# Attention inside a decoder block: the next pair of logit tiles issued ahead of the present pair's transposes, with the interleaving of the gate projection left to the scheduler

## The chip, the cores and the metric

The program runs on one core of one Trainium2 chip. A core has five engines that run their own instruction streams: TensorE (PE, with its weight loads listed as PEld), VectorE (DVE), ScalarE (ACT), GpSimd (POOL) and SyncE (SP), from which this kernel issues its DMAs. The metric is the device time of one execution in microseconds, lower is better.

## The reference

One decoder layer over a sequence of 1024 tokens of width 1024. The normed input is projected once; its columns feed three mixers (RWKV-7, a gated linear recurrence, dilated attention) and three merge gates.

```python
h = rms_norm(x, norm_mix_g)
z_a, z_bx, z_by, z_q, z_k, z_v, z_g = split_cols(h @ w_in, IN_SIZES)   # z_g: 3 * 1024 columns
y_a = rwkv7_mixer(z_a, ...) @ proj_a
y_b = rglru_mixer(z_bx, z_by, ...) @ proj_b
y_c = dilated_attention_mixer(z_q, z_k, z_v, q_g, k_g, rel_bias) @ proj_c
gates = sigmoid(z_g.reshape(bsz, seq, 3, D_MODEL))
x = x + (gates[:, :, 0] * y_a + gates[:, :, 1] * y_b + gates[:, :, 2] * y_c) @ w_out
x = x + square(relu(rms_norm(x, norm_mlp_g) @ mlp_up)) @ mlp_down
```

The attention has three groups g with dilations 1, 4 and 16, each with four heads of 64. A block of 128 queries sees its own 128 keys and the previous 128 of the same residue class.

```python
logits = einsum('brnqhe,brnkhe->brnhqk', qs, kb) + bias      # masked
m = max(logits);  p = exp(logits - m);  l = sum(p)
o = einsum('brnhqk,brnkhe->brnqhe', p, vb) / l;  lse = m + log(l)
# the three groups are then summed with softmax(lse) over the groups as weights
```

## The kernel before, in words

The stages follow one another: norm and projections, the linear recurrence, RWKV (to about 800 us of the profile), the attention together with the gate projection z_g (about 806 to 1140 us), the merge (products named `pj`), output projection, and the MLP. The change touches only the attention with the gate projection.

**Attention.** There are six units `(cc, g)`: two pairs of heads (`cc`) times three groups, in the order cc=0 with g=0,1,2, then cc=1. A unit has four tiles `sp` of 256 queries for two heads `h`. One tile is: the logits `l` on PE (L1029) into one PSUM bank per head; on DVE scale and bias into the SBUF tile `lg` (L1039), the row maxima `stat` (L1042, L1045) and their negation `nm` (L1046); on ACT the exponential in place in `lg` (L1048); on PE 128x128 transposes `pt` of `lg` (L1059); on ACT the copies `ptS` (L1063, L1067); on PE the product `o` with the values `vt` (L1074); on DVE the copy `og` (L1182). In the traces a name carries its indices: `l1110` is g=1, cc=1, sp=1, head 0. A unit's inputs are loaded by `load` (`z0`, `z1`, L998) and `prep` (`bias`, then the broadcast rows `rb`, which scale `z1` at L1012). At a unit's end `combine_rows` transposes the statistics (`stt`, L1083), stores them and reads them back as rows (L1091).

**Combination.** `combine(cc)` weighs and adds the three groups' outputs in halves: small 16-row work for the weights (L1102 to L1120), a store `cw_d` and broadcast loads `cb` (L121), `yc` = weight times og (L1138), `yt` (L1142), and POOL's `yc += yt` (L1143), then the store `yc_d` (L1145). For cc=0 all products run on POOL, during unit (1,0) and after it; for cc=1 they run on DVE at the end. The `yt` tiles use the same two buffers (tag "lg") as the logit tiles.

**Gate projection.** `gate_z` is a generator: each step gives out one product `zg` of twelve 128x512 matmuls (`mm3`, L236 to L238: three fp32r matmuls per k-tile). From the third pair n of column tiles on it uses a Strassen-Winograd scheme: seven products j in two PSUM banks, with operands `wz` made by ACT (L1313) and POOL or DVE (L1314) from the loads `wr_z` (L1293), sums of weights on DVE (L1308 to L1312), the combinations T1 to T4 of the activations (L1244 to L1253), and evacuation by an ACT copy (L1353), a DVE addition `th` (L1357) and a tanh on ACT with a store (L1281, L1282). `th_103` is n=10, j=3.

**Order.** The code is traced in Python, and a scheduler then orders each engine's instructions by a timeline that it simulates. `filler(n)` takes n more steps from `gate_z`; before the change each such step may not be scheduled ahead of the last logits matmul of the third tile back (`tc.issue_after(pins[-lag].ins)`). Buffers that matter: two PSUM banks for `l`, two for `pt`, one each for two `o`; two SBUF buffers for `lg` with `yt`, two for `rb` with `cb`; one each for `z0`, `z1`, `vt`, `bias`.

Of the kernel before, what the change touches and what calls it, by code (L numbers as in the profile page):

```python
# [18 lines left out]
P = 128  # L19
# [13 lines left out]
DILS = (1, 4, 8)  # L33
# [91 lines left out]
def hybrid_block(ctx, tc, io, out, dbg=None):  # L125
    nc = tc.nc
    V, A, G, S, PE = nc.vector, nc.scalar, nc.gpsimd, nc.sync, nc.tensor
    dbg = dbg or {}

    cp = ctx.enter_context(tc.tile_pool(name="cp", bufs=1))  # L130
    wp = ctx.enter_context(tc.tile_pool(name="wp", bufs=1))
    dr = ctx.enter_context(tc.tile_pool(name="dr", bufs=1, space=DRAM))
    pg = ctx.enter_context(tc.tile_pool(name="pg", bufs=2, space=PSUM))
# [192 lines left out]
    gt = gt_p.__enter__()  # L326
    h2_p = tc.tile_pool(name="hS", bufs=1, side="right")
    h2 = h2_p.__enter__()
    late = []
    fill = gate_z(tc, w_in, ht, h2, hp, gt, wp, pg, th_d, load_cols, mm3, late)  # L330
    ys = {}

    def load_y(src, b, ks, place, raw=None):
# [650 lines left out]
    return first  # L984


def attention(tc, io, dbg, psum, der, cg, yc_d, bias_d, sst, rk_d, cw_d, v_d, qk_d, fill):
# [4 lines left out]
    with tc.tile_pool(name="ac", bufs=1) as ac, tc.tile_pool(name="au", bufs=2) as au:  # L992
# [19 lines left out]
                V.scalar_tensor_tensor(kn[:, sl], kn[:, sl], gcol, rb, ALU.mult, ALU.mult)  # L1012
            stats[(cc, g)] = au.tile([P, 2, 2, 8], F32, tag="stat", name=f"stat{u}", bufs=4)

        def tiles(cc, g, sp, po):

            u = f"{g}{cc}"
            dil = DILS[g]
            q_, kn, rqk, vt = zt[(cc, g, 0)], zt[(cc, g, 1)], rqks[(cc, g)], vts[(cc, g)]
            bias, stat = biases[(cc, g)], stats[(cc, g)]  # L1020
            los = [0 if (dil == 1 and s > 0) or (dil == 4 and s % 2 == 1) else 128 for s in (2 * sp, 2 * sp + 1)]
            hs = [slice(64 * h, 64 * h + 64) for h in range(2)]
            same = los[0] == los[1]
            pls = [psum("s", 2, f"l{u}{sp}{h}") for h in range(2)]

            for q in range(2):
                s, lo = 2 * sp + q, los[q]
                for h in range(2):
                    mm = PE.matmul(pls[h][:, 256 * q + lo : 256 * q + 256], q_[hs[h], s * P : (s + 1) * P],  # L1029
                                   kn[hs[h], s * P + lo - 128 : (s + 1) * P], start=True, stop=True)  # L1030
            pins.append(mm)
            lgs = []
            for h in range(2):
                lg = au.tile([P, 2, 256], F32, tag="lg", name=f"lg{u}{sp}{h}")
                lgs.append(lg)
                nm = au.tile([P, 2], F32, tag="nm", name=f"nm{u}{sp}{h}")
                for q in range(2):
                    s, lo = 2 * sp + q, los[q]
                    V.scalar_tensor_tensor(lg[:, q, lo:256], pls[h][:, 256 * q + lo : 256 * q + 256], rqk[:, 8 * h + s : 8 * h + s + 1],  # L1039
                                           bias[:, h, lo:256], ALU.mult, ALU.add)  # L1040
                if same:
                    V.tensor_reduce(stat[:, 0, h, 2 * sp : 2 * sp + 2], lg[:, :, los[0] : 256], AX.X, ALU.max)  # L1042
                else:
                    for q in range(2):
                        V.tensor_reduce(stat[:, 0, h, 2 * sp + q : 2 * sp + q + 1], lg[:, q, los[q] : 256], AX.X, ALU.max)  # L1045
                V.tensor_scalar(nm, stat[:, 0, h, 2 * sp : 2 * sp + 2], -1.0, None, ALU.mult)  # L1046
                for q in range(2):
                    A.activation(lg[:, q, los[q] : 256], lg[:, q, los[q] : 256], AF.Exp, bias=nm[:, q : q + 1],  # L1048
                                 accum_out=stat[:, 1, h, 2 * sp + q : 2 * sp + q + 1])
            yield  # L1050
            ptSs = []
            for h in range(2):
                lg = lgs[h]
                pt = psum("w", 2, f"pt{u}{sp}{h}")
                ptS = au.tile([P, 2, 2, P], F32, tag="ptS", name=f"ptS{u}{sp}{h}")
                ptSs.append(ptS)
                for q in range(2):
                    for b in range(los[q] // 128, 2):
                        PE.transpose(pt[:, 256 * q + 128 * b : 256 * q + 128 * b + 128], lg[:, q, 128 * b : 128 * b + 128], ident)  # L1059
                p4 = pt.rearrange("p (q b t) -> p q b t", q=2, b=2)  # L1060
                if same:
                    b0 = los[0] // 128
                    A.copy(ptS[:, :, b0:2, :], p4[:, :, b0:2, :])  # L1063
                else:
                    for q in range(2):
                        b0 = los[q] // 128
                        A.copy(ptS[:, q, b0:2, :], p4[:, q, b0:2, :])  # L1067

            for q in range(2):
                s = 2 * sp + q  # L1070
                b0 = los[q] // 128
                for b in range(b0, 2):
                    for h in range(2):
                        PE.matmul(po[hs[h], q * P : (q + 1) * P], vt[:, s - 1 + b, hs[h]], ptSs[h][:, q, b, :], start=b == b0, stop=b == 1)  # L1074
# [86 lines left out]
        load(*units[0])
# [56 lines left out]
def gate_z(tc, w_in, ht, h2, hp, gt, wp, pg, th_d, load_cols, mm3, late):  # L1218


    nc = tc.nc
# [13 lines left out]
    def combinations():  # L1235
# [37 lines left out]
        for k in range(4):  # L1273
# [3 lines left out]
            if k % 2:  # L1277
                yield

    def done(b, m, hf, th, src):  # L1280
        A.activation(th, src, AF.Tanh, scale=0.5)  # L1281
        S.dma_start(th_d[b, m, :, hf * H : hf * H + H], th)  # L1282
# [56 lines left out]
    for n in range(n_plain, len(pairs)):  # L1339
# [5 lines left out]
        for j, (nm, bk, first) in enumerate((("B11", X, True), ("B21", Y, True), ("T2", X, False), ("T1", Y, True),  # L1345
# [1 line left out]
            if n == n_plain:  # L1347
                next(comb, None)
            wh, wl = ops.pop((n, j))
            mm3(bk, [(wh[:, k, :], wl[:, k, :], B[nm][0][:, k, :], B[nm][1][:, k, :]) for k in range(4)], first=first, skip=True)  # L1350
            if j in (0, 2, 3):
                t = tile(f"{n}{j}")
                A.copy(t, bk)  # L1353
# [431 lines left out]
```

## Time and profile before

| | |
|---|---|
| runs, us | 1974.58, 1969.91, 1969.65 (median 1969.91) |
| profiled execution, us | 1969.19 |
| its span, us | 1967.2 |
| granted TensorE clock, mean | 0.989 |
| PE busy | 1901.7 us, 97% of the span |
| PEld busy | 1511.0 us, 77% |
| DVE / ACT / POOL busy | 63% / 39% / 39% |

The profile covers one execution; its span lies 2.0 us under that execution's time. A busy share is the engine's time under instructions, and PE's matmuls overlap, so what a stage costs is read from the distance between the starts of matmuls and from PE's waits, not from the durations alone. L numbers are lines of the kernel before; the changed kernel's lines are up to 23 higher in this part.

### The profile page before, as it was taken

Reading aid. Unit: us, or ns where it says so; the run is one execution under the profiler, and the core shown is the slowest. Engines: PE = TensorE matmul, PEld = TensorE weight load, DVE = VectorE, ACT = ScalarE, POOL = GpSimd, SP = SyncE. Lnnn points to the kernel's source line nnn. Section 1 sums busy time; section 2 is a strip of 40 time slices with the busy share of each in tenths; the row PEclk is TensorE's granted clock in tenths of the full one; section 3 lists DMA queues with packets and bytes.
Section 4 is the critical chain, followed back from the end, with each engine's and each line's share of the span. In section 5 each row is a group of like instructions: output and inputs, shape, how many; then the busy total and the mean of one; then the engine's idle time right before and its main releaser. Section 6 shows DMA issues by size and latency. Waiting matters only on the chain. (4 is left out here: it accounts for less than half of the span.)

```text
span 1967.2 us, 29765 instructions
## 1 busy us (share of the span) xinstructions
PE 1901.7 (97%) x11634; PEld 1511.0 (77%) x11634; DVE 1245.2 (63%) x1992; ACT 761.9 (39%) x1275; POOL 773.5 (39%) x631
## 2 busy tenths in 40 slices
PE   8999999999999999999999999998999999999999
PEld 6776777787677878777767778887888888888887
DVE  5546356657656564775454566447776677987975
ACT  5675223233333331355545331145333233333332
POOL 1243424442352350442442352344344343444542
PEclk9999999999999999999999999999999999999999
DMA  4122322221221221424443574442444439535231
GB/s 148 54 61 78 93 52 59 59 60 51 55 70 41 64 66 37 134 92 135 129 147 119 173 267 159 177 172 107 161 150 153 158 141 386 195 133 190 89 129 64
DMA packets 191554, 236.53 MB, mean 120 GB/s; under 512 B 38472, under 2 KB 133349, under 8 KB 191414
## 3 DMA queue, kind: packets, MB, share of 16 engines
q1 hardware_dynamic: 191238, 234.62, 35.9%
q8 instruction: 91, 1.49, 0.3%
q14 instruction: 49, 0.40, 0.1%
q0 software_dynamic: 160, 0.02, 0.0%
q10 hardware_dynamic: 16, 0.00, 0.0%
HBM read 168.14 MB, written 68.82 MB: 120 GB/s over the span
## 5 line engine op out<-in xcount | busy, mean ns | idle before, releaser
L1505 POOL TENSOR_TENSOR wl_d<-dr,wh_d 128x1024 fp32r<-128x1024 f32 x40 | 101.3, 2532 | 126.9 <-ACT wh_d L1504 118.4
L1314 POOL TENSOR_TENSOR wz<-wr_z,wz 128x512 fp32r<-128x512 f32 x60 | 80.6, 1344 | 161.8 <-ACT wz L1313 147.6
L1505 DVE TENSOR_TENSOR du<-dq,du 128x1024 fp32r<-128x1024 f32 x56 | 126.1, 2251 | 23.3 <-ACT du L1504 22.7
L236 PE MATMUL dx<-wh_d,du 128*128 128x512 f32 x256 | 99.7, 389 | 0.4 <-DVE acc L1685 0.4
L237 PE MATMUL dx<-wl_d,du 128*128 128x512 f32 x256 | 99.6, 389 | 0.0
L238 PE MATMUL dx<-wh_d,du 128*128 128x512 f32 x256 | 99.4, 389 | 0.0
L1504 ACT CAST wh_d<-dr 128x1024 fp32r<-128x1024 f32 x40 | 42.1, 1052 | 141.7 <-PE dx L238 72.8
L788 DVE TENSOR_SCALAR s<-ac,wc 64x64 f32<-64x64 f32 x128 | 36.1, 282 | 66.7 <-PE ac L784 64.4
L1505 POOL TENSOR_TENSOR wl_a<-ur,wh_a 128x1024 fp32r<-128x1024 f32 x15 | 47.6, 3174 | 75.3 <-ACT wh_a L1504 75.3
L237 PE MATMUL g_z<-hl,wh_z 128*128 128x512 f32 x192 | 77.1, 402 | 0.0
L238 PE MATMUL g_z<-hh,wl_z 128*128 128x512 f32 x192 | 76.9, 401 | 0.0
L236 PE MATMUL g_z<-hh,wh_z 128*128 128x512 f32 x192 | 76.5, 398 | 0.4 <-DVE zsq L443 0.4
L1505 POOL TENSOR_TENSOR wl_s<-ur,wh_s 128x1024 fp32r<-128x1024 f32 x16 | 43.3, 2704 | 77.7 <-ACT wh_s L1504 77.7
L229 POOL TENSOR_TENSOR wl_wo<-wr_wo,wh_wo 128x1024 fp32r<-128x1024 f32 x16 | 38.7, 2416 | 62.6 <-ACT wh_wo L228 62.6
L1504 ACT CAST du<-dq 128x1024 fp32r<-128x1024 f32 x56 | 58.6, 1047 | 1.8 <-DMA dq<-u_d 1.8
L1048 ACT ACTIVATE lg<-lg,nm 128x128 f32<-128x128 f32 (+1 forms) x96 | 42.3, 443 | 42.0 <-DVE nm L1046 42.0
L1685 DVE TENSOR_TENSOR acc<-dx,acc 128x512 f32<-128x512 f32 x64 | 41.9, 679 | 25.1 <-PE dx L238 25.1
L236 PE MATMUL v<-wh_wv,hh 128*128 128x256 f32 x192 | 56.3, 293 | 1.2 <-DVE st L794 1.2
L236 PEld LDWEIGHTS dx<-wh_d,du 128*128 128x128 f32 x256 | 48.0, 188 | 10.8 <-DVE acc L1685 0.9
L238 PEld LDWEIGHTS dx<-wh_d,du 128*128 128x128 f32 x256 | 48.1, 188 | 10.1
L237 PEld LDWEIGHTS dx<-wl_d,du 128*128 128x128 f32 x256 | 48.0, 188 | 9.9
L237 PE MATMUL v<-wl_wv,hh 128*128 128x256 f32 x192 | 55.6, 290 | 0.0
(757 smaller groups left out, 6178.7 us busy)
## 6 DMA issues: line engine op xcount, KB each, us to landing
dq<-u_d SPq DMA_DIRECT2D x56, 512.0 KB
wr_z<-in_w_in_dram SPq DMA_DIRECT2D x32, 512.0 KB
ur<-in_mlp_up_dram SPq DMA_DIRECT2D x16, 1024.0 KB
dr<-in_mlp_down_dram SPq DMA_DIRECT2D x16, 1024.0 KB
th_d<-th SPq DMA_DIRECT2D x48, 256.0 KB
tg<-th_d SPq DMA_DIRECT2D x32, 256.0 KB
wr_wo<-in_w_out_dram SPq DMA_DIRECT2D x16, 512.0 KB
qk_d<-zo SPq DMA_DIRECT2D x24, 256.0 KB
```

What stands on the lines that cost most here:

```text
L229: E.tensor_tensor(lo, raw, hi, ALU.subtract)
L236: PE.matmul(ps, lh, rh, start=first and i == 0, stop=False, skip_group_check=skip)
L237: PE.matmul(ps, lh, rl, start=False, stop=False, skip_group_check=skip)
L238: end = PE.matmul(ps, ll, rh, start=False, stop=last and i == n - 1, skip_group_check=skip)
L788: V.tensor_scalar(ns[half[h], :], pb[h][half[h], 128 * j + 64 * c : 128 * j + 64 * c + 64], wc[half[h], 2 * i + c : 2 * i + c + 1], None, ...
L1048: A.activation(lg[:, q, los[q] : 256], lg[:, q, los[q] : 256], AF.Exp, bias=nm[:, q : q + 1], accum_out=stat[:, 1, h, 2 * sp + q : 2 * sp ...
L1314: (V if i == 2 else G).tensor_tensor(l, src, h, ALU.subtract)
L1504: A.copy(hi, src)
L1505: split.last = E.tensor_tensor(lo, src, hi, ALU.subtract)
L1685: V.tensor_tensor(acc[row][:, half[col]], ps, acc[row][:, half[col]], ALU.add)
```

## The change

The generator `tiles` is split into three functions. `logits(cc, g, sp)` holds the `l` matmuls, the DVE work and the exponentials, and leaves its `lg` tiles in a dictionary; `transposes` takes both `pt` banks and gives out all transposes before the copies `ptS`; `values` holds the `o` products. The loop traces `logits` of tile sp+1 ahead of `transposes` of tile sp. `load` and `prep` of the next unit move from behind tile 3 to behind the transposes of tile 2. `combine(0)` is made before the tile loop of unit (1,0) rather than behind its first tile. `filler` no longer pins its steps; it takes 2 steps at a unit's start, 1.2 behind each tile's transposes and 1.4 behind each of the first three `o` products, where it was 2 + 0.2 a tile and 3 at a unit's end. The dictionary `order` and the context `in_order()` are empty and record only the last matmul.

```diff
-        def filler(n, lag=3):
+        def filler(n):
             nonlocal owed
             owed += n
             while owed >= 1:
                 owed -= 1
-                with tc.issue_after(pins[-lag].ins) if len(pins) >= lag else nullcontext():
-                    next(fill, None)
+                next(fill, None)
...
+            logits(cc, g, 0)
+            filler(2)
+            if n == 3:
+                sums = combine(0)
             for sp in range(4):
-                po = psum(f"ac{sp % 2}", 1, f"o{g}{cc}{sp}")
-                for i, _ in enumerate(tiles(cc, g, sp, po)):
-                    filler(0.2 if i else 2)
-                    next(sums, None)
-                    next(sums, None)
-                V.tensor_copy(ogs[(cc, g)][:, sp * 256 : (sp + 1) * 256], po[:, 0:256])
-                if sp == 3 and n + 1 < 6:
+                if sp + 1 < 4:
+                    logits(cc, g, sp + 1)
+                ptSs = transposes(cc, g, sp)
+                if sp == 2 and n + 1 < 6:
                     load(*units[n + 1])
                     prep(*units[n + 1])
-                    filler(3)
-                if sp == 0 and n == 3:
-                    sums = combine(0)
+                filler(1.2)
+                next(sums, None)
+                po = psum(f"ac{sp % 2}", 1, f"o{g}{cc}{sp}")
+                values(cc, g, sp, ptSs, po)
+                V.tensor_copy(ogs[(cc, g)][:, sp * 256 : (sp + 1) * 256], po[:, 0:256])
+                if sp < 3:
+                    filler(1.4)
+                next(sums, None)
+                next(sums, None)
...
+        def transposes(cc, g, sp):
...
+            pts = [psum("w", 2, f"pt{u}{sp}{h}") for h in range(2)]
+            with in_order():
+                for h in range(2):
+                    for q in range(2):
+                        for b in range(los[q] // 128, 2):
+                            order["block"] = PE.transpose(pts[h][:, 256 * q + 128 * b : 256 * q + 128 * b + 128], lgs[sp][h][:, q, 128 * b : 128 * b + 128], ident)
```

Both programs hold the same number of matmuls. In the attention, PE's order before has 286 runs of one kind of matmul: 45 of `l`, 41 of `o`, 59 of `pt`, 134 of `zg` and 7 others. In the new order there are 252: 39, 36, 47, 123 and 7. Three places show what moves.

PE in unit (1,1), where the logits of its last tile `l113*` meet the values `o111` of its second tile. Before:

```order
L1074 MATMUL o111_9909<-ptS1110_9974,vt11_9819 64x128
L238 MATMUL zg70_9847<-hh11_95,wz75_9804 128x512
L1029 MATMUL l1130_10077<-z1_11_9740,z0_11_9738 128x128
L1029 MATMUL l1130_10077<-z1_11_9740,z0_11_9738 128x256
L1059 MATMUL pt1120_10055<-cg_102,lg1120_10001 128x128
L236 MATMUL zg71_9848<-zT4h_8485,wz76_9863 128x512
L237 MATMUL zg71_9848<-zT4l_8486,wz76_9863 128x512
L238 MATMUL zg71_9848<-zT4h_8485,wz76_9863 128x512
L1059 MATMUL pt1120_10055<-cg_102,lg1120_10001 128x128 x2
L236 MATMUL zg71_9848<-zT4h_8485,wz76_9863 128x512
L1029 MATMUL l1131_10078<-z1_11_9740,z0_11_9738 128x128
L1074 MATMUL o111_9909<-ptS1111_9981,vt11_9819 64x128
```

After, from the first `o111` that stands together with others:

```order
L1088 MATMUL o111_9971<-ptS1111_9950,vt11_9743 64x128
L1088 MATMUL o111_9971<-ptS1110_9947,vt11_9743 64x128
L1088 MATMUL o111_9971<-ptS1111_9950,vt11_9743 64x128
L1088 MATMUL o111_9971<-ptS1110_9947,vt11_9743 64x128
L1088 MATMUL o111_9971<-ptS1111_9950,vt11_9743 64x128
L1038 MATMUL l1131_10019<-z1_11_9595,z0_11_9593 128x128
L1038 MATMUL l1131_10019<-z1_11_9595,z0_11_9593 128x256
L1067 MATMUL pt1121_10043<-cg_102,lg1121_9930 128x128 x3
L236 MATMUL zg70_9892<-hh11_95,wz75_9881 128x512
L237 MATMUL zg70_9892<-hl11_96,wz75_9881 128x512
L238 MATMUL zg70_9892<-hh11_95,wz75_9881 128x512
L236 MATMUL zg70_9892<-hh11_95,wz75_9881 128x512
```

The logits and values that stood one or two at a time between `zg` matmuls now stand in longer runs, and the transposes `pt112*` of the third tile follow in fewer pieces.

DVE in the same unit, around the weight sum that needs the load `wr_z80` (L1308 and L1309 before, L1331 and L1332 after). Before:

```order
L1357 TENSOR_TENSOR th_70_9861<-zg70_9847,th_70_9861 128x512
L1039 SCALAR_TENSOR_TENSOR lg1110_9916<-l1110_9910,sst_84,bias11_9742 128x128
L1039 SCALAR_TENSOR_TENSOR lg1110_9916<-l1110_9910,sst_84,bias11_9742 128x256
L1308 TENSOR_TENSOR wr_z80_9866<-wr_z81_9868,wr_z80_9866 128x512
L1045 TENSOR_REDUCE stat11_9752<-lg1110_9916 128x1
L1039 SCALAR_TENSOR_TENSOR lg1111_9925<-l1111_9911,sst_84,bias11_9742 128x128
L1045 TENSOR_REDUCE stat11_9752<-lg1110_9916 128x1
L1039 SCALAR_TENSOR_TENSOR lg1111_9925<-l1111_9911,sst_84,bias11_9742 128x256
L1309 TENSOR_TENSOR wr_z81_9868<-wr_z81_9868 128x512
```

After:

```order
L1047 SCALAR_TENSOR_TENSOR lg1110_9816<-l1110_9810,sst_84,bias11_9597 128x128
L1047 SCALAR_TENSOR_TENSOR lg1110_9816<-l1110_9810,sst_84,bias11_9597 128x256
L1053 TENSOR_REDUCE stat11_9607<-lg1110_9816 128x1 x2
L1054 TENSOR_SCALAR nm1110_9817<-stat11_9607 128x2
L1380 TENSOR_TENSOR th_70_9906<-zg70_9892,th_70_9906 128x512
L1331 TENSOR_TENSOR wr_z80_9911<-wr_z81_9913,wr_z80_9911 128x512
L1332 TENSOR_TENSOR wr_z81_9913<-wr_z81_9913 128x512
L1047 SCALAR_TENSOR_TENSOR lg1111_9825<-l1111_9811,sst_84,bias11_9597 128x128
L1047 SCALAR_TENSOR_TENSOR lg1111_9825<-l1111_9811,sst_84,bias11_9597 128x256
```

The maxima and `nm` of `lg1110` now stand ahead of the sum that needs `wr_z80`; `lg1111` stands behind both sums.

DVE at the end of the attention, where `combine(1)` (`yc`, `yt`) meets the evacuations `th_100`, `th_103`, `th_102` of n=10. Before:

```order
L1357 TENSOR_TENSOR th_100_10626<-zg101_10613,th_100_10626 128x512
L1308 TENSOR_TENSOR wr_z110_10631<-wr_z111_10633,wr_z110_10631 128x512
L1309 TENSOR_TENSOR wr_z111_10633<-wr_z111_10633 128x512
L1138 TENSOR_TENSOR yc10_10713<-cb10_10661,og01_9318 128x512
L1311 TENSOR_TENSOR th_s11_10708<-wr_z110_10631,wr_z111_10633 128x512
L1312 TENSOR_TENSOR wr_z110_10631<-wr_z110_10631,th_s11_10708 128x512
L1142 TENSOR_TENSOR yt101_10733<-cb11_10666,og11_9818 128x512
L1314 TENSOR_TENSOR wz112_10705<-th_s11_10708,wz112_10705 128x512
L1357 TENSOR_TENSOR th_103_10703<-zg100_10612,th_103_10703 128x512
L1142 TENSOR_TENSOR yt102_10754<-cb12_10671,og21_10264 128x512
L1142 TENSOR_TENSOR yt111_10797<-cb11_10666,og11_9818 128x512
L1357 TENSOR_TENSOR th_102_10686<-zg101_10613,th_102_10686 128x512
```

After:

```order
L1380 TENSOR_TENSOR th_100_10647<-zg101_10634,th_100_10647 128x512
L1151 TENSOR_TENSOR yc10_10674<-cb10_10620,og01_9259 128x512
L1155 TENSOR_TENSOR yt101_10693<-cb11_10625,og11_9742 128x512
L1155 TENSOR_TENSOR yt102_10718<-cb12_10630,og21_10166 128x512
L1155 TENSOR_TENSOR yt111_10760<-cb11_10625,og11_9742 128x512
L1155 TENSOR_TENSOR yt112_10781<-cb12_10630,og21_10166 128x512
L1380 TENSOR_TENSOR th_103_10708<-zg100_10633,th_103_10708 128x512
L1331 TENSOR_TENSOR wr_z110_10652<-wr_z111_10654,wr_z110_10652 128x512
L1151 TENSOR_TENSOR yc11_10740<-cb10_10620,og01_9259 128x512
L1332 TENSOR_TENSOR wr_z111_10654<-wr_z111_10654 128x512
L1334 TENSOR_TENSOR th_s11_10713<-wr_z110_10652,wr_z111_10654 128x512
L1380 TENSOR_TENSOR th_102_10688<-zg101_10634,th_102_10688 128x512
```

`th_103` stood behind the weight sums of `wr_z110`, one `yc` and one `yt`; now it stands behind one `yc` and four `yt`, of which the last two wait for POOL to free a buffer, and the weight sums follow it.

On POOL the thirteen instructions from `yt001` to the last `yc01` addition keep their kinds. On SP the loads `cb010` and `cb011`, which stood ahead of the store of `th_60`, now stand behind it; the load `wr_z80`, with five DMAs between it and the store of `yc01` before, now follows that store directly; and both loads `wr_z110` and `wr_z111`, which stood around the first store `cw_d` of `combine(1)`, now follow all its stores `cw_d` and loads `cb`; the last store `cw_d`, which stood behind four `cb` loads, now stands ahead of them.

More of the change, by code (lines that the diff above doesn't have):

```diff
@@ L328, in hybrid_block @@
     h2 = h2_p.__enter__()
-    late = []
-    fill = gate_z(tc, w_in, ht, h2, hp, gt, wp, pg, th_d, load_cols, mm3, late)
+    late, order = [], {}
+    fill = gate_z(tc, w_in, ht, h2, hp, gt, wp, pg, th_d, load_cols, mm3, late, order)
     ys = {}
@@ L369, in hybrid_block @@
     late.append(load_first)
-    attention(tc, io, dbg, psum, der, cg, yc_d, bias_d, sst, rk_d, cw_d, v_d, qk_d, fill)
+    attention(tc, io, dbg, psum, der, cg, yc_d, bias_d, sst, rk_d, cw_d, v_d, qk_d, fill, order)
     yp_p = tc.tile_pool(name="yp", bufs=1)
@@ L984, in lru, with attention @@
     return first
-def attention(tc, io, dbg, psum, der, cg, yc_d, bias_d, sst, rk_d, cw_d, v_d, qk_d, fill):
+def attention(tc, io, dbg, psum, der, cg, yc_d, bias_d, sst, rk_d, cw_d, v_d, qk_d, fill, order):
     nc = tc.nc
@@ L1049, in tiles @@
                                  accum_out=stat[:, 1, h, 2 * sp + q : 2 * sp + q + 1])
-            yield
+        def transposes(cc, g, sp):
+            u = f"{g}{cc}"
+            los, hs, same = places(g, sp)
+            pts = [psum("w", 2, f"pt{u}{sp}{h}") for h in range(2)]
+            with in_order():
+                for h in range(2):
+                    for q in range(2):
+                        for b in range(los[q] // 128, 2):
+                            order["block"] = PE.transpose(pts[h][:, 256 * q + 128 * b : 256 * q + 128 * b + 128], lgs[sp][h][:, q, 128 * b : 128 * b + 128], ident)
@@ L1051, in tiles @@
             ptSs = []
             for h in range(2):
-                lg = lgs[h]
-                pt = psum("w", 2, f"pt{u}{sp}{h}")
                 ptS = au.tile([P, 2, 2, P], F32, tag="ptS", name=f"ptS{u}{sp}{h}")
                 ptSs.append(ptS)
-                for q in range(2):
-                    for b in range(los[q] // 128, 2):
-                        PE.transpose(pt[:, 256 * q + 128 * b : 256 * q + 128 * b + 128], lg[:, q, 128 * b : 128 * b + 128], ident)
-                p4 = pt.rearrange("p (q b t) -> p q b t", q=2, b=2)
@@ L1061, in tiles @@
[L1061 to L1074, printed above, removed]
@@ L1075, in tiles, with values @@
-            yield
+                p4 = pts[h].rearrange("p (q b t) -> p q b t", q=2, b=2)
+                for q in ([slice(0, 2)] if same else range(2)):
+                    b0 = los[0 if same else q] // 128
+                    A.copy(ptS[:, q, b0:2, :], p4[:, q, b0:2, :])
+            return ptSs
+        def values(cc, g, sp, ptSs, po):
+            los, hs, same = places(g, sp)
+            vt = vts[(cc, g)]
+            with in_order():
+                for q in range(2):
+                    s = 2 * sp + q
+                    b0 = los[q] // 128
+                    for b in range(b0, 2):
+                        for h in range(2):
+                            order["block"] = PE.matmul(po[hs[h], q * P : (q + 1) * P], vt[:, s - 1 + b, hs[h]], ptSs[h][:, q, b, :], start=b == b0, stop=b == 1)
@@ L1215, in bias_tiles, with gate_z @@
             S.dma_start(bias_d[g], bass.AP(tensor=src.tensor, offset=src.offset, ap=[[EW, 4], [0, P], [1, EW]]))
-def gate_z(tc, w_in, ht, h2, hp, gt, wp, pg, th_d, load_cols, mm3, late):
+def gate_z(tc, w_in, ht, h2, hp, gt, wp, pg, th_d, load_cols, mm3, late, order):
     nc = tc.nc
@@ L1278, in combinations, with products @@
                 yield
+    def products(*args, **kw):
+        with nullcontext():
+            order["fill"] = mm3(*args, **kw)
     def done(b, m, hf, th, src):
@@ L1327, in gate_z @@
                 for kh in range(2):
-                    mm3(ps, [(hi[:, 4 * kh + k, :], lo[:, 4 * kh + k, :], ht[(0, kh, hf)][:, k, :], ht[(1, kh, hf)][:, k, :]) for k in range(4)],
-                        first=kh == 0, last=kh == 1)
+                    products(ps, [(hi[:, 4 * kh + k, :], lo[:, 4 * kh + k, :], ht[(0, kh, hf)][:, k, :], ht[(1, kh, hf)][:, k, :]) for k in range(4)],
+                             first=kh == 0, last=kh == 1)
                     next(comb, None)
@@ L1349, in gate_z @@
             wh, wl = ops.pop((n, j))
-            mm3(bk, [(wh[:, k, :], wl[:, k, :], B[nm][0][:, k, :], B[nm][1][:, k, :]) for k in range(4)], first=first, skip=True)
+            products(bk, [(wh[:, k, :], wl[:, k, :], B[nm][0][:, k, :], B[nm][1][:, k, :]) for k in range(4)], first=first, skip=True)
             if j in (0, 2, 3):
```

29 lines of the change are left out of this document (15 added, 14 removed).

## Prediction

> **What bounds the kernel now.** I read the busy shares first, then the attention's stretch cut into windows, then PE's waits in it, then single matmuls.
>
> ```profile
> PE 1901.7 (97%) x11634; PEld 1511.0 (77%) x11634; DVE 1245.2 (63%) x1992; ACT 761.9 (39%) x1275; POOL 773.5 (39%) x631
> ```
>
> PE is the bound of the whole program. The change can only give back time in which PE stands, or in which it runs less densely than it could, between 806 and 1140 us. The windows' columns are PE, PEld, DVE, ACT and POOL busy, granted clock, DMA share and rate:
>
> ```profile
> 868.00:877.00 9.00, 7.42 (x41) 5.26 (x40) 9.00 (x19) 5.51 (x12) 2.26 (x2) 1.00 0.43 117
> 877.00:1001.00 124.00, 124.00 (x645) 91.30 (x645) 65.87 (x150) 66.43 (x185) 52.31 (x46) 1.00 0.43 136
> 1001.00:1004.00 3.00, 2.24 (x20) 1.45 (x16) 2.26 (x3) 0.51 (x2) 3.00 (x3) 1.00 0.09 34
> 1015.00:1020.00 5.00, 3.49 (x23) 2.16 (x21) 1.24 (x1) 3.02 (x8) 2.54 (x2) 1.00 0.64 177
> 1020.00:1028.00 8.00, 6.38 (x18) 4.65 (x19) 6.67 (x19) 3.46 (x13) 0.00 (x0) 0.57 0.00 1
> 1028.00:1099.00 71.00, 71.00 (x364) 52.61 (x363) 33.98 (x87) 36.71 (x105) 20.78 (x16) 1.00 0.34 105
> 1099.00:1118.00 19.00, 14.36 (x62) 10.92 (x61) 12.08 (x17) 5.95 (x11) 7.79 (x6) 1.00 0.49 140
> 1130.00:1138.00 8.00, 5.57 (x18) 4.16 (x17) 7.07 (x4) 8.00 (x11) 6.83 (x3) 0.79 1.04 402
> ```
>
> For 195 us (the second and sixth row) PE is never idle. The rest holds its losses; those behind the names of their releasers (total, times, longest, 800 to 1142 us) are small:
>
> ```profile
> PE zg L236 <- DVE th L1357: 5.4, 4, 1.8
> PE l L1029 <- DVE lg L1039: 3.9, 2, 2.7
> PE zg L236 <- ACT th L1353: 2.4, 1, 2.4
> PE o L1074 <- ACT ptS L1067: 1.2, 2, 0.8
> PE l L1029 <- DVE z L1012: 0.8, 1, 0.8
> ```
>
> So all of PE's waits together are about 14 us, and a gain of the order of 10 us is what can be had here.
>
> **Fewer changes between kinds of matmul.** Even without idle time PE loses something when a block of `o` or `l` stands between `zg` matmuls:
>
> ```profile
> 1040.27 0.39 PE L237 MATMUL zg<-hl,wz 128*128 128x512 f32 x1
> 1040.49 0.39 PE L238 MATMUL zg<-hh,wz 128*128 128x512 f32 x1
> 1040.81 0.88 PE L1074 MATMUL o<-ptS,vt 128*64 128x128 f32 x12
> 1041.62 0.50 PE L236 MATMUL zg<-hh,wz 128*128 128x512 f32 x1
> 1041.95 0.39 PE L237 MATMUL zg<-hl,wz 128*128 128x512 f32 x1
> ...
> 1093.73 0.39 PE L238 MATMUL zg<-hh,wz 128*128 128x512 f32 x1
> 1094.05 0.65 PE L1074 MATMUL o<-ptS,vt 128*64 128x128 f32 x6
> 1094.63 0.50 PE L236 MATMUL zg<-hh,wz 128*128 128x512 f32 x1
> 1094.97 0.40 PE L237 MATMUL zg<-hl,wz 128*128 128x512 f32 x1
> ```
>
> Undisturbed, `zg` starts follow at 0.22 to 0.23 us. From the last `zg` before a block to the second one behind it are two such steps, 0.45 us. With twelve `o` between them it took 1041.95 - 1040.49 = 1.46 us, so the block cost 1.01 us; with six it took 1.24 us, 0.79 us. Six more matmuls cost 0.22 us, 0.04 each, which leaves 0.55 us for a block as such. Some of that is the ordinary price of the first matmuls; I take 0.45. The order counts 45 runs of `l` and 41 of `o` before, 39 and 36 after: 11 blocks fewer, **-5.0 us**. The bounds are 0 (the blocks that vanish stood beside others anyway) and 11 x 0.55 = -6.1. The loads of weights say the same:
>
> ```profile
> L1029 PEld LDWEIGHTS l<-z,z 64*128 64x128 f32 x192 | 20.8, 188 | 16.5 <-issue 8.4 <-DVE lg L1039 5.2 <-DVE z L1012 1.2
> L1074 PEld LDWEIGHTS o<-ptS,vt 128*64 128x64 f32 x280 | 18.1, 136 | 14.7 <-issue 8.5 <-ACT ptS L1067 1.9 <-ACT lg L1048 1.7
> ```
>
> The weight loads of `l` and `o` stood for 8.4 and 8.5 us without any cause that the profile shows ("issue"), about 0.2 us for each of 86 blocks. [...]
>
> **The stall at 872.** PE is idle for 1.58 of the 9 us from 868 to 877 (0.8 in `o`, waiting for ACT's `ptS`, and 0.7 in `zg`, waiting for DVE's `th`), and against a dense order it loses 2.3. DVE is busy for all 9 us: the four T4 sums stand as one block ahead of the `lg` work and `th_20`. In the new order `lg101*` stands after half of the sums and `th_20` between the others, while PE has the logits of the next tile already. I leave 0.5 for `th_20`: **-1.8 us** (bounds 0 and -2.3).
>
> **The stall at 1002.** `l` waits for DVE's `z`, whose `rb` loads were late on SP. With `load` and `prep` a tile earlier this wait goes: **-1.0 us** (0.8 idle and the restart; bounds 0 and -1.0). The same move shortens the cover between a unit's last `l` and the next unit's first, over which `z0` and `z1` are reloaded; I count 8 to 10 us of matmuls there in the new order. No stall is put down.
>
> **Unit (1,1), 1015 to 1028.** Here PE idles 1.51 and 1.62 us, and then runs at a granted clock of 0.57 for 8 us; against a dense order the two windows lose 6.2 us. The cause is DVE's order: the sum of `wr_z80` stands ahead of the `lg111*` work.
>
> ```profile
> DVE wr_z L1308 <- DMA wr_z<-in_w_in_dram: 13.4, 6, 5.7
> ...
> 979.60 3.11 POOL L1142 TENSOR_TENSOR yt<-cb,og 128x512 f32<-128x512 f32 x2 [1.98 <-PE pt L1059]
> ...
> 1002.74 1.71 POOL L1143 TENSOR_TENSOR yc<-yc,yt 128x512 f32<-128x512 f32 x1
> ```
>
> The 5.7 us wait is the one. In the new order `lg1110` is through before that sum. A new dependence comes in: `combine(0)` now uses the two `lg` buffers between `lg013*` and `lg110*`, so the first logits of unit (1,1) wait for POOL's last additions. POOL took 979.60 to 1004.45, 24.9 us, for that sequence. In the new order I count, with 0.227 us a `zg` matmul, 0.1 us another and 0.45 us a block, 24.3 us from `pt0130`, which frees the first buffer, to `l1111`, which needs `lg1101` to have read its bank. With 0.9 us for the two `lg1101` operations the stall is 24.9 + 0.9 - 24.3 = 1.5 us; I add 1.0 for `lg1111` behind the `wr_z80` sums, so 6.2 becomes 2.5: **-3.7 us** (bounds -6.2, and +10.4 in a rival below).
>
> **The end of the attention, 1099 to 1118.** PE loses 4.6 us in three waits for `th`, 5.5 against a dense order.
>
> ```profile
> 1099.91 1.57 DVE L1120 TENSOR_TENSOR cw<-cw,mx 16x128 f32<-16x128 f32 x2
> 1101.41 0.67 DVE L1357 TENSOR_TENSOR th<-zg,th 128x512 f32<-128x512 f32 x1
> 1104.42 1.25 DVE L1308 TENSOR_TENSOR wr_z<-wr_z,wr_z 128x512 f32<-128x512 f32 x1 [2.33 <-DMA wr_z<-in_w_in_dram]
> ...
> 1108.03 0.69 DVE L1138 TENSOR_TENSOR yc<-cb,og 128x512 f32<-128x512 f32 x1 [1.64 <-DMA cb<-cw_d]
> ...
> 1110.04 1.06 DVE L1142 TENSOR_TENSOR yt<-cb,og 128x512 f32<-128x512 f32 x1
> ...
> 1114.51 2.02 DVE L1142 TENSOR_TENSOR yt<-cb,og 128x512 f32<-128x512 f32 x2 [2.21 <-DMA cb<-cw_d]
> ...
> 1111.18 1.65 POOL L1143 TENSOR_TENSOR yc<-yc,yt 128x512 f32<-128x512 f32 x1 [6.06 <-DVE yt L1142]
> 1115.73 1.94 POOL L1143 TENSOR_TENSOR yc<-yc,yt 128x512 f32<-128x512 f32 x1 [1.65 <-DVE yt L1142]
> ...
> 1089.65 0.33 SPq L1086 DMA_DIRECT2D st_d<-st  x1
> ```
>
> From the statistics' store (1089.65, behind `stt`, 0.6 us after its start) to the first `yc` (1108.03) are 18.4 us, so 19.0 from `stt`. In the new order `th_103` follows one `yc` and four `yt`, two of which wait for POOL's additions: 0.69 + 1.06 + 1.65 + 1.94 + 1.06 + 0.67 = 7.1 us. From `stt` to the product that needs `th_103` to have emptied its bank I count 8 products of 2.73 us, 21.9. The stall is 19.0 + 7.1 - 21.9 = 4.2 us. `th_102` then stands behind the sums of `wr_z110` and one `yc`, about 4.0 us of DVE work with itself against one product of 2.7: 1.3. `th_100` no longer waits. Behind a long stall the clock is lower. The windows bound what that costs: at 1130 5.57 us of work ran at 0.79, which is 5.57 x 0.21 = 1.2 us lost; at 1020 the 6.2 us lost, less the 3.1 us of idle time in its two windows, leave 3.1. I take 1.7, nearer to the row at 1130, which is free of `l` and `o` blocks. So 4.2 + 1.3 + 1.7 = 7.2 for 5.5: **+1.7 us** (bounds -5.5, and +5.8 in a rival below).
>
> **What stays.** The wait at 1130 (`zg` behind ACT, 2.4 us, clock 0.79) belongs to the loads for the merge. The work of `gate_z` that is taken inside the loop is 70 products for 72; the rest runs behind it, at the same price. `transposes` takes both `pt` banks at once; no wait for them appears in the rows above, and with the logits a tile ahead PE has other matmuls.
>
> **Sum.** -5.0 - 1.8 - 1.0 - 3.7 + 1.7 = -9.8 us on the profiled execution's 1969.19 (span 1967.2), which lies 0.7 under the median: 1959.4.
>
> **Rivals.** *The hand-over of the `lg` buffers decides (slower).* On SP the loads `cb010` and `cb011` now stand behind the store of `th_60`, which waits for ACT's tanh.
>
> ```profile
> SPq L1282 <- ACT th L1281: 103.3, 29, 13.4
> ```
>
> Such a store held SP for up to 13.4 us, 3.6 in the mean of 29. If POOL's sequence starts 13.4 us later, unit (1,1) stalls for 1.5 + 13.4 = 14.9 us and 1.7 for the clock, 16.6 where 6.2 was: +10.4 in place of -3.7, in all +4.3, **1973.5**. Slower at all it is from a delay of 9.1 us on, by over 0.3% from 15. Against it: the mean wait, and that PE's products feed that tanh without a wait. *The last `cb` comes as late as before.* The second `yt` started 6.5 us after the first `yc` (1114.51). With that, `th_103` ends 6.5 + 1.06 + 1.94 + 1.06 + 0.67 = 11.2 us after it, 4.1 more: **1963.5**. For it speaks that three loads share the queue; against it that the last store `cw_d` now precedes them. *The blocks cost nothing as such.* Then only stalls move: **1964.4**. [...] That the order stays as it was is excluded by the counts of runs.
>
> **How the numbers follow.** The forecast has 0.55; the late `cb` 0.14; free blocks 0.13; the hand-over 0.13; 0.05 are for stalls that vanish altogether (down to 1950). A measurement of this kernel tells about 0.3%, 5.9 us, from no change. Below 1963.3 lie nine tenths of the first case, under half of the second and third, and the last: 0.64. Above 1975.1 lie some 0.4 of the hand-over and a little of the rest: 0.10. Within: 0.26. The likeliest case alone spans 1954 to 1964. The range for 8 in 10 takes in the late `cb`, free blocks and most of the hand-over: 1953 to 1971.
>
> **What would show it.** PE's wait for `lg` with 2.7 us and the clock of 0.57 near 1020 should be gone; the one for `z` too; the stretch from 868 to 877 should show PE nearly full. One wait of `zg` for `th` of about 4 us should appear near the end, with a slower clock behind it. If the idle time goes and the time does not, the price of a block is wrong; if `l` waits for `lg` at the start of unit (1,1) for more than 5 us, the hand-over is.

## The result, and the profile after

The changed kernel takes 1959.34 us in the median of 7 runs (1956.15 to 1962.84), the kernel before 1970.83 (1966.37 to 1974.58, 7 runs). The ratio is 0.9938 with a 95% interval of 0.9922 to 0.9954: 0.6% faster, by more than the 0.3% that can be told from no change. The profiled execution took 1960.56 us, its span is 1958.5.

PE's waits from 800 to 1142 us after the change (total, times, longest):

```profile
PE zg L236 <- DVE th L1380: 6.0, 2, 5.6
PE zg L236 <- ACT th L1376: 3.6, 1, 3.6
PE l L1038 <- DVE lg L1047: 1.2, 1, 1.2
PE pt L1067 <- ACT lg L1056: 1.0, 2, 0.7
```

The wait of `l` for `lg` with 2.7 us, the one for `z`, and `o`'s waits for `ptS` are gone. One wait for `th` of 5.6 us has taken the place of three of 4.6 in all, and the last wait of the stage has grown from 2.4 to 3.6 us. The same by windows (PE, PEld, DVE, ACT, POOL busy, granted clock, DMA share, rate):

```profile
868.00:880.00 12.00, 12.00 (x63) 8.65 (x62) 12.00 (x25) 7.39 (x22) 4.10 (x3) 1.00 0.36 103
1001.00:1028.00 27.00, 27.00 (x141) 19.16 (x139) 17.77 (x46) 16.67 (x54) 8.55 (x7) 1.00 0.43 142
1094.00:1102.00 8.00, 2.44 (x10) 1.73 (x9) 5.84 (x6) 1.77 (x3) 6.49 (x4) 0.74 0.62 191
1102.00:1107.00 5.00, 4.93 (x16) 3.63 (x16) 5.00 (x7) 2.45 (x5) 4.03 (x3) 0.74 0.14 52
1119.00:1124.00 5.00, 1.45 (x6) 0.89 (x5) 3.37 (x2) 5.00 (x6) 3.05 (x2) 0.77 1.04 392
1124.00:1131.00 7.00, 7.00 (x23) 5.52 (x22) 3.31 (x4) 4.21 (x7) 7.00 (x3) 0.68 1.04 390
```

PE is full from 868 to 880 and from 1001 to 1028, where the stalls were. Nearly all that is left stands in two places, 1094 to 1107 and 1119 to 1131, each a wait with a slower clock behind it.

To compare kernels I use the stretch from the first logits to the last merge product (`pj`), which holds the same matmuls in all kernels of the table: 435.8 us before, 425.6 after, 10.2 less. In front of it the profiled execution of the changed kernel takes 0.9 us longer than the one before, and behind it 0.5 us longer. The stretch is split in three: the sum of the distances between starts of neighbouring matmuls, each pair of kinds at the distance that it has when nothing waits ("steps"); the excess of single distances over 0.5 us ("waits"); and the rest, which is the slower clock and small waits.

| kernel, us | stretch | steps | waits | rest |
|---|---|---|---|---|
| before | 435.8 | 413.2 | 15.7 | 7.0 |
| after | 425.6 | 409.3 | 12.1 | 4.2 |
| logits ahead alone (below) | 426.4 | 409.0 | 10.9 | 6.4 |
| all but logits ahead | 436.0 | 414.2 | 12.2 | 9.6 |
| four `yt` buffers | 425.2 | 409.3 | 11.5 | 4.4 |
| `th` first | 415.0 | 409.3 | 4.0 | 1.7 |
| `th` and copy first | 412.5 | 409.4 | 2.8 | 0.2 |

The border between steps and rest depends on which distance is taken as the usual one. With the median over these seven kernels, for each pair of kinds and shapes, the steps fall by 2.3 us from before to after and not by 3.9, and the rest falls by 4.2. The rest also holds a chance part: in "logits ahead alone" and in "`th` first" the granted clock is 0.50 for 3.4 us from 826 on, behind a wait of 1.2 us of `l` for `lg`; the changed kernel has the same wait, and its profiled execution keeps the full clock there.

### The profile page after: what moved, and what is told of

It is laid out like the page before. It is cut to its first block, busy times and chain, and to the rows that moved or that the text cites. A ratio compares the mean times of both kernels' runs of the same rounds, so it can differ in the third digit from the quotient of the medians.

```text
span 1958.5 us, 29762 instructions
## 1 busy us (share of the span) xinstructions
PE 1896.8 (97%) x11634; PEld 1511.5 (77%) x11634; DVE 1244.5 (64%) x1992; ACT 760.4 (39%) x1275; POOL 776.9 (40%) x631
## 4 chain that ended last, share of the span: by engine, by line
PE 77%; DVE 8%; DMA 6%; ACT 3%; issue 2%; POOL 2%; SPq 1%; DVEq 0%; POOLq 0%; ACTq 0%
PE zg L236 3%; PE zg L238 3%; PE zg L237 3%; PE dx L236 3%; PE dx L237 3%; PE dx L238 3%; PE ux L236 2%; PE ux L237 2%; PE ux L238 2%; PE g_z L237 2%; PE g_z L236 2%; PE g_z L238 2%; PE pj L237 2%; PE pj L236 2%; PE pj L238 2%
## 5 line engine op out<-in xcount | busy, mean ns | idle before, releaser
L238 PE MATMUL v<-wh_wv,hl 128*128 128x256 f32 x192 | 56.5, 295 | 0.0
L236 PEld LDWEIGHTS dx<-wh_d,du 128*128 128x128 f32 x256 | 48.1, 188 | 10.9 <-DVE acc L1708 0.9
```

The source lines that it names most:

```text
L236: PE.matmul(ps, lh, rh, start=first and i == 0, stop=False, skip_group_check=skip)
L238: end = PE.matmul(ps, ll, rh, start=False, stop=last and i == n - 1, skip_group_check=skip)
```

## Experiments: which part of the change carries it

**The logits ahead alone.** The changed kernel with the two moves undone; the new fill steps and the transposes taken together stay:

```diff
-            if n == 3:
-                sums = combine(0)
...
-                if sp == 2 and n + 1 < 6:
-                    load(*units[n + 1])
-                    prep(*units[n + 1])
                 filler(1.2)
...
                 if sp < 3:
                     filler(1.4)
+                elif n + 1 < 6:
+                    load(*units[n + 1])
+                    prep(*units[n + 1])
...
+                if sp == 0 and n == 3:
+                    sums = combine(0)
```

> The changed kernel with load and prep of the next unit back behind tile 3, and combine(0) back behind the first tile: the logits a tile ahead alone. If these carry the block count and the order on DVE, the stretch keeps its gain but for the 1.0 us wait for z: about 1960. If the two other moves removed the stall of unit (1,1), it comes back with some 4 to 6 us: about 1964 to 1966.

1959.99 us (ratio to before 0.9956, 0.9939 to 0.9973); the stretch is 426.4 us, 0.8 longer than after the whole change. Neither the stall of unit (1,1) nor the wait for `z` came back: on top of the logits ahead the two moves carry next to nothing.

**All but the logits ahead.** The kernel before, with the moves and the new fill steps:

```diff
+            if n == 3:
+                sums = combine(0)
             for sp in range(4):
...
-                    filler(0.2 if i else 2)
+                    filler(1.4 if i else 1.2)
                     next(sums, None)
-                    next(sums, None)
+                    if i:
+                        next(sums, None)
...
-                if sp == 3 and n + 1 < 6:
+                if sp == 2 and n + 1 < 6:
                     load(*units[n + 1])
                     prep(*units[n + 1])
-                    filler(3)
-                if sp == 0 and n == 3:
-                    sums = combine(0)
```

> The kernel before with the rest of the change and without the logits ahead: load and prep behind tile 2, combine(0) made ahead of unit (1,0), fill steps 1.2 and 1.4. Runs of logits and values rise from 86 to 92. If the logits ahead carry the gain, this is no faster than before: 1970, or 1972 with 6 more blocks. If the moves and the fill steps carry a part, the waits at 1002 and in unit (1,1) go: about 1964.

1969.95 us, ratio 1.0007 (0.9991 to 1.0022): no change. It is not that nothing moved. The stall of unit (1,1) is gone here too (PE busy 29.46 of the 30 us from 1000 to 1030), but the steps grew by 1.0 us with 6 more blocks, and the end got worse:

```profile
PE zg L236 <- DVE th L1357: 5.9, 3, 3.7
PE zg L236 <- ACT th L1353: 1.8, 1, 1.8
PE l L1029 <- DVE z L1012: 1.1, 1, 1.1
```

The wait for `z` that the earlier `prep` was to remove is there (1.1 us). About half of the rest of 9.6 us (half of 3.4 us, three times) went in three stretches of 3.4 us at a granted clock of 0.50, from 986 (behind the wait for `z`), 1092 and 1109 (behind waits for `th`); the execution before keeps the full clock at these places. So the stall of unit (1,1) can be removed in two ways; fewer blocks come from the logits ahead alone.

The last part, the pin on `filler`, needed no run: the changed kernel with `tc.issue_after` put back, and the kernel before without it, hold the same instructions in the same order on all five engines as without that edit. The pin bound nothing.

## Experiments: what a block costs

**PE's order written out, in whole blocks and with the values split.** Both kernels chain each block behind the product traced ahead of it and each half product behind the block; the second also puts half a product between the two halves of the values, as the added `filler(0.5)` shows (the first takes it behind the copy `og`). The lines that cut the products and the steps of `filler` in halves are left out here.

```diff
         def in_order():
-            return nullcontext()
+            return tc.issue_after(order["fill"].ins) if "fill" in order else nullcontext()
...
-                values(cc, g, sp, ptSs, po)
+                values(cc, g, sp, ptSs, po, (0,))
+                filler(0.5)
+                values(cc, g, sp, ptSs, po, (1,))
...
-        with nullcontext():
+        with tc.issue_after(order["block"].ins) if "block" in order else nullcontext():
             order["fill"] = mm3(*args, **kw)
```

> The changed kernel with PE's order written out in the attention: each group of logits, of transposes and of values stands whole, and the gate products follow in halves of six matmuls; both halves of the values are one block. Runs of logits and values fall from 75 to 55. If a block costs 0.45 us as such, the stretch from the first logits to the first merge product loses 20 x 0.45 = 9.0 us of non-idle time (about 1950 us in all, plus the waits that a fixed order brings). If blocks are free, it takes as long as in the changed kernel but for its own waits (1959).

> As the run before (order written out), but half a gate product stands between the two halves of the values, so that there are 24 more runs of logits and values (79) with the same matmuls. If a block costs 0.45 us as such: 24 x 0.45 = 10.8 us longer than the run before. If blocks are free: the same within 2 us, but for waits that the profile names.

Both missed by far: 1978.13 us (ratio 1.0043, 1.0026 to 1.0059) and 1979.90 (1.0057, 1.0038 to 1.0076), stretches of 443.7 and 445.4 us. (These stretches hold 24 more gate matmuls, 5.4 us: the changed kernel runs them ahead of its first logits, where PE waits for 5.4 us here.) PE's waits in the first:

```profile
PE zg L236 <- DVE th L1386: 10.8, 5, 5.9
PE pt L1067 <- ACT lg L1056: 10.1, 4, 3.3
PE l L1038 <- issue: 5.4, 1, 5.4
PE l L1038 <- DVE lg L1047: 3.9, 2, 3.0
```

30.4 us of waits, against 11.8 after the change: a fixed order of whole blocks leaves PE nothing to do while ACT's exponentials and DVE's `th` catch up. What 20 blocks fewer save, some 7 us at the price found below, is lost more than twice over. With the waits in the way the total can't price a block, but a single place can. First the whole block, then the split one:

```profile
895.80 0.39 PE L238 MATMUL zg<-hh,wz 128*128 128x512 f32 x1
896.12 0.88 PE L1088 MATMUL o<-ptS,vt 128*64 128x128 f32 x12
896.92 0.50 PE L236 MATMUL zg<-hh,wz 128*128 128x512 f32 x1
897.26 0.39 PE L237 MATMUL zg<-hl,wz 128*128 128x512 f32 x1
```

```profile
895.33 0.39 PE L238 MATMUL zg<-hh,wz 128*128 128x512 f32 x1
895.64 0.44 PE L1088 MATMUL o<-ptS,vt 128*64 128x128 f32 x4
896.01 0.50 PE L236 MATMUL zg<-hh,wz 128*128 128x512 f32 x1
896.35 0.39 PE L237 MATMUL zg<-hl,wz 128*128 128x512 f32 x1
...
897.27 0.40 PE L238 MATMUL zg<-hh,wz 128*128 128x512 f32 x1
897.60 0.66 PE L1088 MATMUL o<-ptS,vt 128*64 128x128 f32 x8
898.19 0.50 PE L236 MATMUL zg<-zT4h,wz 128*128 128x512 f32 x1
898.52 0.39 PE L237 MATMUL zg<-zT4l,wz 128*128 128x512 f32 x1
```

Less two `zg` steps (0.45), twelve `o` cost 1.01 us in one block; in two they cost 0.57 and 0.80. One more block is 0.36 us.

**The price by itself.** The fastest version below has almost no waits. To it I added 28 unused matmuls (two records each in the trace) of the shape of the values, in one block (28 behind product j=1 of n=11) and in fourteen (two behind each product of n=10 and 11):

```diff
     def products(*args, **kw):
-        with nullcontext():
+        with tc.issue_after(order["spare"].ins) if "spare" in order else nullcontext():
...
+            if extra.get((n, j)):
+                with tc.issue_after(order["fill"].ins):
+                    pd = order["psum"]("s", 2, f"pd{n}{j}")
+                    for i in range(extra[(n, j)]):
+                        order["spare"] = nc.tensor.matmul(pd[0:64, 0:128], order["ident"][:, 0:64], order["ident"], start=i == 0, stop=i == extra[(n, j)] - 1)
```

> The fastest version so far (copy th_113 first) with work added: 28 unused 64x128 matmuls of the shape of the values (56 records in the trace) in one block between two products of the last pair. At 0.05 us a record and 0.35 us a block the stretch to the end of the merge products grows by 3.2 us; if a block as such is free, by 2.8 us.

> The same 28 added matmuls as 14 blocks of two, one behind each product of the last two pairs. At 0.35 us a block as such 13 x 0.35 = 4.6 us more than the run before; at the 0.45 us of the prediction 5.9 us more; if blocks are free, the same within 1 us.

One block: 1956.49 us; fourteen: 1960.74, that is 4.25 more, where 4.6 was expected at 0.35 us a block, 5.9 at 0.45 and less than 1 if blocks are free. The stretches are 420.0 and 423.7. The size of the added work was wrong, though: one block grew the stretch by 7.5 us over 412.5, not 3.2. Its rows say why, first of the one block, then of the first of fourteen:

```profile
1105.69 0.39 PE L238 MATMUL zg<-hh,wz 128*128 128x512 f32 x1
1106.01 6.33 PE L1381 MATMUL pd<-cg 128*64 128x128 f32 x56
1112.27 0.50 PE L236 MATMUL zg<-zT2h,wz 128*128 128x512 f32 x1
1112.61 0.40 PE L237 MATMUL zg<-zT2l,wz 128*128 128x512 f32 x1
```

```profile
1079.18 0.39 PE L238 MATMUL zg<-hh,wz 128*128 128x512 f32 x1
1079.50 0.65 PE L1381 MATMUL pd<-cg 128*64 128x128 f32 x4
1080.08 0.50 PE L236 MATMUL zg<-hh,wz 128*128 128x512 f32 x1
1080.42 0.40 PE L237 MATMUL zg<-hl,wz 128*128 128x512 f32 x1
```

56 records cost 6.92 - 0.45 = 6.47 us and four cost 1.24 - 0.45 = 0.79: 0.11 a record and 0.35 a block. The remaining 1.0 us of the 7.5 lies in small waits. The fourteen blocks have almost none (14 x 0.79 = 11.1 of the 11.2 us by which their stretch exceeds 412.5), so the stretches differ by 3.7 us only, 0.29 a block. It is the rows that give 0.35; the totals exclude free blocks and lean against 0.45.

The kernel's own `o` records are cheaper than the added ones, and the traces show how. Blocks of 2, 4, 6 and 8 `o` records (kernel before, split kernel) cost 0.57, 0.57, 0.79 and 0.79 us, blocks of 10, 12, 14 and 16 cost 1.00, 1.01, 1.22 and 1.23. So one matmul of a head, two records, costs the same 0.22 us with or without the other head's matmul beside it, and 0.35 us stay for the block. The two heads write different halves of the partitions, and the added matmuls all write the same half into one sum; which of the two matters wasn't tried.

Four and 56 added records, and four and twelve of `o`, thus give the same price, 0.35 to 0.36 us; both kinds have 64 columns. For `l`, six of the eleven blocks, the rows of the changed kernel give 0.39: a block of four 64x128 records (at 898) costs 0.62 us and one of eight (at 1037) 0.85, 0.23 for four more.

## Experiments: the end of the attention

After the change DVE's rows there are:

```profile
1090.78 0.69 DVE L1151 TENSOR_TENSOR yc<-cb,og 128x512 f32<-128x512 f32 x1 [5.04 <-DMA cb<-cw_d]
1092.97 1.10 DVE L1155 TENSOR_TENSOR yt<-cb,og 128x512 f32<-128x512 f32 x1 [1.50 <-DMA cb<-cw_d]
1095.07 2.24 DVE L1155 TENSOR_TENSOR yt<-cb,og 128x512 f32<-128x512 f32 x2 [0.99 <-DMA cb<-cw_d]
1098.47 2.07 DVE L1155 TENSOR_TENSOR yt<-cb,og 128x512 f32<-128x512 f32 x1 [1.16 <-POOL yc L1156]
1100.47 0.67 DVE L1380 TENSOR_TENSOR th<-zg,th 128x512 f32<-128x512 f32 x1
```

`th_103` (1100.47) stands behind one `yc` and four `yt`, which wait three times for `cb` and once for POOL. Its own product, whose last matmul started at 1092.53 and took 0.39 us, had ended 7.5 us before.

**Four buffers for `yt`.** `tag="ptS" if cc and g == 2 else "lg"`, nothing else.

> The changed kernel, with the second weighted output of each half of combine(1) in the two buffers of ptS, so that the last two no longer wait for POOL's additions. If that wait is what makes th_103 late, it ends about 2 us earlier, PE's longest wait for th falls from 5.6 to 3.5 us, and the time to about 1957. If the landing of the cb loads sets it, the wait stays at 5 us or more and the time at 1959.

1961.41 us (ratio 0.9964, 0.9942 to 0.9986), no faster than the change, where 1957 was expected. PE's longest wait for `th` did fall from 5.6 to 3.5 us, but another wait took its place:

```profile
PE zg L236 <- DVE th L1380: 4.0, 2, 3.5
PE zg L236 <- ACT wz L1336: 2.8, 1, 2.8
PE zg L236 <- ACT th L1376: 1.8, 1, 1.8
```

The weights of the next pair (`wz`) were late as well, since their loads stand behind six `cb` loads on SP. POOL's buffers were one of two limits a few us apart.

**`th` first, loads first.** Two products are traced with each step of `combine(1)`, and its `yt` are held behind `th` (`order["th104"]` is the instruction that writes `th_103`, `order["th105"]` the one that writes `th_102`):

```diff
-                        E.tensor_tensor(as_nat(t, g), ...)
+                        with tc.issue_after(order["th105" if hf else "th104"].ins) if cc else nullcontext():
+                            E.tensor_tensor(as_nat(t, g), ...)
...
         for _ in combine(1):
-            filler(1)
+            filler(2)
...
-                V.tensor_tensor(t, bk, t, ALU.add)
+                order[f"th{n}{j}"] = V.tensor_tensor(t, bk, t, ALU.add)
```

> The changed kernel with two edits at the end of the attention: two gate products instead of one are traced with each step of combine(1), so that the loads wr_z110 and wr_z111 stand ahead of the cb loads, and the yt of combine(1) are held behind th_103 (first half) and th_102 (second half) on DVE. If the order on DVE and SP is what makes PE wait for th (5.6 us and a slower clock behind it), that wait and the clock's dip go: about 7 us less, 1952. If the next limit is as near as with four yt buffers (a wait of 2.8 us for wz came in its place), 1957.

1949.19 us (1947.93 to 1950.54; ratio to before 0.9899, 0.9881 to 0.9917), about 10 us less than the change and more than the 7 expected. The two edits were not run apart. With the wait and its slow clock the next ones shrank:

```profile
PE zg L236 <- ACT th L1377: 1.7, 1, 1.7
PE zg L236 <- DVE th L1381: 1.2, 2, 0.8
```

**The copy first.** In the change ACT's copy `th_113` stands behind four casts of merge inputs:

```profile
1118.88 1.99 ACT L340 CAST y1T2h<-yr1h 128x1024 fp32r<-128x1024 f32 x2 [3.91 <-DMA yr1h<-yb_d]
1120.78 1.99 ACT L340 CAST y1T1h<-yr1l 128x1024 fp32r<-128x1024 f32 x2
1122.67 0.57 ACT L1376 COPY th<-zg 128x512 f32<-128x512 f32 x1
```

`elif j == 1: late[0]()` became `elif j == 3`, so that the casts are traced behind the copy.

> As the run before, and the loads for the merge are traced behind the fourth product of the last pair rather than the second, so that ACT's copy th_113 stands ahead of the four casts that wait for the load yr1h. If ACT's order makes the last wait of the stage (3.6 us and a slower clock), it goes too: about 5 us less than the run before, 1947. If the first merge products need those casts anyway, the wait moves to them: 0 to 2 us less.

1944.97 us (1943.53 to 1945.75; ratio to before 0.9877, 0.9856 to 0.9898), 4.2 less than the run before and 1.2% faster than the kernel before; PE's longest wait in the stage is 1.1 us. It beats both kernels.

## Why the prediction was right, point by point

The direction, the places and most of the mechanism were right. That the forecast was 1959.4 and the median is 1959.34 is luck: several terms were off and cancelled, and against the forecast of 9.8 us the two profiled executions lie 8.6 apart, the two medians 11.5 and the stretches 10.2.

| term | predicted | measured |
|---|---|---|
| 11 blocks fewer | -5.0 | -3.9 (steps) |
| stall at 872 | -1.8 | -1.8 |
| stall at 1002 | -1.0 | -0.8 |
| unit (1,1) | -3.7 | -6.2 |
| end of the attention | +1.7 | +2.6 |
| last wait of the stage | 0 | +2.1 |
| not named (what remains) | 0 | -2.2 |
| stretch | -9.8 | -10.2 |

The measured terms are the differences of the waits at each place with the clock's loss behind them: 1.0 + 0.8 us at 872; 0.8 at 1002; 0.5 + 2.8 and 2.9 for the clock in unit (1,1); at the end 1.2 + 1.9 + 2.0 before against 5.7 and 2.0 for the clock; at the last wait 2.6 and 1.6 against 3.7 and 2.6. The clock's loss is what the matmuls behind the wait took more than their usual distances.

- *Blocks.* That a block has a price of its own is shown by several sizes of three kinds of block; the step that failed is "I take 0.45" for the block as such. Five `o` blocks at 0.35 and six `l` blocks at 0.39 make 4.1 us, near the 3.9 of the steps; by medians these give 2.3, so the total is less certain than the price. Fitting a block of twelve and one of six gave 0.55, because six records cost as much as eight (0.79 us both; four cost 0.57, twelve 1.01, sixteen 1.22): the slope came out as 0.04 for 0.054. Four and sixteen give 0.35. The rival that blocks are free falls for `l` and `o`, the matmuls of half height and half width. For the transposes it holds: in before one cost 0.12 us in most places, four 0.45 and eight 0.88, with no price for the block. What makes the kinds differ was not tried.
- *Unit (1,1).* The stall went altogether. The step that was mis-sized is POOL's sequence, taken as 24.9 us:

```profile
982.21 1.55 POOL L1155 TENSOR_TENSOR yt<-cb,og 128x512 f32<-128x512 f32 x1 [2.55 <-DMA cb<-cw_d]
...
1000.65 1.29 POOL L1156 TENSOR_TENSOR yc<-yc,yt 128x512 f32<-128x512 f32 x1
...
996.73 0.74 DVE L1047 SCALAR_TENSOR_TENSOR lg<-l,sst,bias 128x128 f32<-128x128 f32 x2 [2.02 <-POOL yc L1156]
1001.97 0.74 DVE L1047 SCALAR_TENSOR_TENSOR lg<-l,sst,bias 128x128 f32<-128x128 f32 x2 [2.50 <-POOL yc L1156]
```

It took 982.21 to 1001.94, 19.7 us; it began 2.6 us late, on a load `cb` and not on `pt0130`. The new dependence is real: DVE waited 2.0 and 2.5 us for POOL to free a buffer. PE did not, as `l1111` started at 1004.69, about 2 us after `lg1101`. The 1.0 us for `lg1111` behind the `wr_z80` sums did not come either: it ran at 1010.70, and PE had other matmuls. The slower rival failed for this margin, and since the store of `th_60` held SP for only 0.5 us.
- *The end.* Place and cause were right. Predicted were 4.2 and 1.3 us, measured one wait of 5.6 and none for `th_102`: from `yc` to the end of `th_103` it took 1101.14 - 1090.78 = 10.4 us, not 7.1, because the second and third `cb` landed later than the first (2.5 us of waits) and the last `yt` took 2.07 us, not 1.06. That is the rival "the last `cb` comes as late as before" by half. Against it the first `yc` came 17.2 us after `stt` (1073.58), not 19.0; 17.2 + 10.4, less the 22.1 us of products that PE had in between, gives the wait. The clock behind it cost 2.0 us where 1.7 was taken.
- *What stays.* This step failed: the last wait did not stay but grew by 1.1 us, and the clock behind it by 1.0. The cause was right: the copy stands behind four casts, and these waited 3.9 us for the load `yr1h`, where it was 2.8 before. Why that load landed later isn't shown. When `th` came first, the wait fell to 1.7 us without another edit.

## What to carry to other kernels

Price a change of order in three parts: the distance between matmuls of neighbouring kinds (here 0.35 us for a block of `o` and 0.39 for one of `l`), the named waits, and the clock behind long waits (here 1.6 to 2.9 us behind waits of 2.4 to 5.6). Issuing a dependent stage one tile ahead paid because blocks merged and DVE's work came earlier, while a fully fixed order with still fewer blocks ended 19 us slower through its waits. Where a stage ends, look at what stands ahead of the evacuation that frees a bank: there three small edits, 14.4 us less than the change together, were worth more than the whole change with its 11.5.

## What the runs showed of the hardware

PE's clock was halved in or behind some idle times of 1.16 to 5.55 us, and not behind others. Rows behind a wait, granted clock third from the end. The first two are of before (PE idle for 2.70 and 1.83 us), then after (5.55), all but logits ahead (1.80) and logits ahead alone (1.16, with the `l` block that follows it):

```profile
1021.60:1023.60 2.00, 1.98 (x5) 1.33 (x6) 1.92 (x6) 1.07 (x5) 0.00 (x0) 0.50 0.00 0
1117.20:1119.20 2.00, 2.00 (x9) 1.66 (x10) 1.49 (x1) 1.60 (x3) 1.73 (x2) 1.00 0.34 132
```

```profile
1101.20:1103.20 2.00, 2.00 (x5) 1.61 (x6) 2.00 (x3) 0.61 (x1) 0.72 (x2) 0.50 0.27 108
```

```profile
1091.40:1093.40 2.00, 2.00 (x5) 1.61 (x6) 1.14 (x4) 1.74 (x3) 0.81 (x1) 0.55 0.07 16
```

```profile
826.60:829.80 3.20, 3.20 (x9) 2.43 (x9) 3.20 (x7) 0.02 (x1) 3.20 (x3) 0.50 0.21 82
```

In before and after, the waits of 2.4 us and more in this stage were all followed by half the clock, for 3 to 6 us behind the wait, at a price of 1.6 to 3 us. Of the waits of about 1.8 us two were (the fourth row, and one at 1126 with four `yt` buffers) and others were not (1.76 and 1.83 in before, with the clock at 1.00 behind them); in the last row one of 1.16 us was, with the matmuls of half height behind it. Outside the stage even 3.06 us (before, 148.89 to 151.95) left the clock at 1.00. The half clock in this stage lasted 3.41 us or 6.83 (before: 6.83 from 1020.60 on, 3.41 from 1133.24 on; after: 6.83 from 1097.82 and from 1121.71 on), and within each of these two executions its beginnings lie a whole multiple of 3.413 us apart (33 and 7 of them). Whether the place of a wait on this grid decides is not shown: no run moved a wait to try it. At these four places the wait and the clock's loss together cost 1.35 to 2 times the wait alone (2.8 + 2.9, 2.6 + 1.6, 5.7 + 2.0 and 3.7 + 2.6 us).
